# Gated delta heads: decay masks, decayed keys and the rounding of weights on other engines

## The chip, the cores and the metric

The kernel runs on one core of a Trainium2 chip. The metric is the device time of one execution in microseconds (us): the median of 3 runs. Names of engines: PE is TensorE (PEld its weight loads), DVE VectorE, ACT ScalarE, POOL GpSimd, SP SyncE, which issues the DMAs.

## The reference

Two transformer blocks in a row on 1024 tokens of width 1024. The first has neighbourhood attention beside a gated delta rule in both directions; the second has stick-breaking attention beside retention. The change touches the delta rule of the first block, whose core is this:

```python
def _gated_delta_chunked(q, k, v, g, beta):
    g = jnp.cumsum(g, axis=-1)                      # within a chunk
    diff = g[..., :, None] - g[..., None, :]
    decay = jnp.where(tri, jnp.exp(jnp.where(tri, diff, 0.0)), 0.0)
    a_mat = jnp.where(strict, jnp.einsum('bhncd,bhnsd->bhncs', kb, k) * decay, 0.0) + eye
    ...
    intra = jnp.einsum('bhncd,bhnsd->bhncs', q, k) * decay
    ...
    S = S * jnp.exp(g_last) + jnp.einsum('bhcd,bhce->bhde',
                                         k_c * jnp.exp(g_last[..., None] - g_c)[..., None], v_new)
```

The kernel works it in chunks of 128 tokens. There are 4 heads of 128 columns and two directions (`d` is 0 or 1), so 8 pairs, called `dh`.

## The kernel before, in words

All large products are in 32-bit floats split in two: a rounded part (`hi`, float32r) and the residue (`lo`), three matmuls for one product (`PASSES`). Weights come from HBM in units of 128 rows: `split_unit` loads a unit into `raw` (3 slots), writes the rounded part to `wu[:, 0]` (line 70, on POOL) and the residue to `wu[:, 1]` (line 71, on POOL). `wu` has 10 slots; a group of weights is 8 units (`load_units`).

The program is written as one function and put in order by a list scheduler of the framework, which models the engines' times and writes out one fixed order for each engine and for the DMA queue on SP. An engine runs its order strictly in sequence and waits at the head of it.

First come the norm of the input, its transposes (`h1hi`, `h1lo`) and the gates, ending in `gc`, the sum of the log decays within a chunk by token (`[P, 8, NM]`, P = 128 partitions, NM = 8 chunks), and its transposed copy in DRAM, `d_g`.

Then the loop over 4 delta heads (lines 304 to 435), the stage of the change. For a head: 8 units of 3 x 128 columns of weights (line 308); three products with the input (`dense_col`, line 112), each in two halves that ACT copies to `pad` (line 315); the convolution of five taps on DVE (lines 318, 320); silu on ACT (line 323); norms and transposes to `kt`, `vt`, `kT` (lines 327 to 356). For each direction, `G` is the row of the sums, broadcast to all partitions by a DMA (line 370); `el` is the decay to the end of the chunk. The inner function `decay` makes a mask of 128 x 8 x 128: the difference of `G` and the token's own sum (DVE, line 385), the triangle by an affine select (POOL, line 386), the exponential (ACT, line 389). E0, E2 and E1 are such masks; E2 and E1 share a buffer. N (line 406) and IT (line 421) are products of masks with the keys' and queries' products in PSUM, sent to DRAM (`d_N`, `d_pk`). Last, `G` becomes its exponential in place (line 427), and three scaled tiles per direction go to `d_pk`: lines 430 (DVE and POOL) and 434 (DVE, keys times `el`). Their buffers `sct` are two, shared with `vt`.

After the heads a triangular solver in 62 steps runs on DVE and POOL (lines 463, 465), with the neighbourhood attention on PE beside it; then the merges of the solutions, the scan over chunks, and the output product (line 859, from about 740 us). The second block follows.

Of the kernel before, what the change touches and what calls it, by code (L numbers as in the profile page):

```python
# [11 lines left out]
F32 = mybir.dt.float32  # L12
F32R = mybir.dt.float32r
AF = mybir.ActivationFunctionType
ALU = mybir.AluOpType
# [4 lines left out]
P = 128  # L20
# [16 lines left out]
def tile_kernel(ctx: ExitStack, tc: tile.TileContext, I: dict, out: bass.AP, dbg=None, stop=None):  # L37
# [22 lines left out]

    def split_unit(src, ncol, pool=None, tag="wu", parts=1, fast=False, rpool=None):
        raw = (rpool or wraw).tile([P, ncol], F32, tag="raw", name="raw", bufs=8 if rpool else 3)
        dst = raw if parts == 1 else raw.rearrange("p (g c) -> p g c", g=parts)
        nc.sync.dma_start(out=dst, in_=src)
        u = (pool or wpool).tile([P, 2, ncol], F32R, tag=tag, name="wu")
        if fast:
            nc.scalar.copy(out=u[:, 0, :], in_=raw)
            nc.vector.tensor_tensor(out=u[:, 1, :], in0=raw, in1=f32(u[:, 0, :]), op=ALU.subtract)
        else:
            nc.gpsimd.tensor_scalar(out=u[:, 0, :], in0=raw, scalar1=1.0, scalar2=0.0, op0=ALU.mult, op1=ALU.add)  # L70
            nc.gpsimd.tensor_tensor(out=u[:, 1, :], in0=raw, in1=f32(u[:, 0, :]), op=ALU.subtract)  # L71
        return u

    def load_units(w, c0, width, parts=1, stride=0, pool=None, tag="wu", fast=False, rpool=None):
        us = []
        for k in range(NK):
            rows = w[k * P:(k + 1) * P, :]
            if parts == 1:
                src = rows[:, c0:c0 + width]
            else:  # L80
                src = rows[:, c0:c0 + parts * stride].rearrange("p (g s) -> p g s", g=parts)[:, :, :width]
            us.append(split_unit(src, width * parts, pool, tag, parts, fast and k % 2 == 1, rpool))
        return us
# [3 lines left out]
    def bank(tag, w=512):  # L87
        if tag == "a":
            return psA.tile([P, w], F32, tag="a", name="acc")
        return psB.tile([P, w], F32, tag=tag, name="p" + tag, bufs=2 if tag == "z" else 1)  # L90
# [195 lines left out]
    nc.tensor.matmul(pg[:, 32:64], lhsT=trige, rhs=graw[:, 4:8, :], start=True, stop=True)  # L286
    nc.vector.tensor_copy(out=gc, in_=pg[:, 0:64])
    pgt = bank("z")
    nc.tensor.transpose(pgt[:64, 0:P], gc.rearrange("p a b -> p (a b)"), ident)
# [14 lines left out]
    for h in range(4):  # L304
        kt = dn.tile([P, NM, P], F32, tag="kt", name="kt")
        vt = dn.tile([P, NM, P], F32, tag="sct", name="vt", bufs=2)
        kT = dn.tile([P, T], F32, tag="kT", name="kT")
        us = load_units(I["w_in"], 2048 + 128 * h, 128, parts=3, stride=512)
        sT = []
# [57 lines left out]
        for d in range(2):  # L367
# [7 lines left out]
            nc.scalar.activation(out=el[:, dh, :], in_=el[:, dh, :], func=AF.Exp)  # L375
            gb = gc[:, dh, :].unsqueeze(2).to_broadcast([P, NM, P])
            bb = beta[:, dh, :].unsqueeze(2).to_broadcast([P, NM, P])
# [4 lines left out]

            def decay(a, b, sgn, strict, tag):
                E = dn.tile([P, NM, P], F32, tag=tag, name="E")
                nc.vector.tensor_tensor(out=E, in0=a, in1=b, op=ALU.subtract)
                nc.gpsimd.affine_select(out=E, in_=E, pattern=[[0, NM], [sgn, P]],
                                        compare_op=ALU.is_gt if strict else ALU.is_ge, fill=NEG,
                                        base=0, channel_multiplier=-sgn)
                nc.scalar.activation(out=E, in_=E, func=AF.Exp)
                return E  # L390

            if d == 0:
                E0 = decay(G, gb, 1, False, "E0")
                nc.vector.tensor_tensor(out=E0, in0=E0, in1=bb, op=ALU.mult)
            else:
                E2 = decay(gb, G, 1, True, "E1")
                nc.vector.tensor_tensor(out=E2, in0=E2, in1=bb, op=ALU.mult)
                for g in range(2):
# [5 lines left out]
                    for dd_, E in enumerate((E0, E2)):  # L404
# [4 lines left out]
                        for x, (r_, c_) in enumerate(((0, 0), (64, 64), (0, 64))):  # L409
                            nc.sync.dma_start(out=d_N[x, a_:a_ + 4].rearrange("n r c -> r n c"),  # L410
                                              in_=N[r_:r_ + 64, :, c_:c_ + 64])
                E1 = decay(G, gb, -1, False, "E1")
                for g in range(2):
# [11 lines left out]
        for d in range(2):  # L425
            dh, G = d * 4 + h, Gs[d]
            nc.scalar.activation(out=G, in_=G, func=AF.Exp)
            for f, src in enumerate((kT, sT[0])):
                sc_t = dn.tile([P, NM, P], F32, tag="sct", name="sct", bufs=2)
                (nc.gpsimd if f else nc.vector).tensor_tensor(out=sc_t.rearrange("p n c -> p (n c)"), in0=src, in1=G.rearrange("p n c -> p (n c)"),  # L430
                                        op=ALU.mult)
                nc.sync.dma_start(out=d_pk[d, :, :, f, h, :].rearrange("n p c -> p n c"), in_=sc_t)
            sc_t = dn.tile([P, NM, P], F32, tag="sct", name="sct", bufs=2)
            nc.vector.tensor_tensor(out=sc_t, in0=kt, in1=el[:, dh, :].unsqueeze(2).to_broadcast([P, NM, P]), op=ALU.mult)
            nc.sync.dma_start(out=d_pk[d, :, :, 2, h, :].rearrange("n p c -> p n c"), in_=sc_t)
# [898 lines left out]
```

## Time and profile before

| | us |
|---|---|
| median of 3 runs | 2325.04 (2324.49 to 2326.11) |
| profiled execution | 2327.74 |
| its span, first to last instruction | 2326.0 |
| PE busy in the span | 2189.8 (94%) |
| DVE / ACT / POOL busy | 1270.2 / 892.9 / 1205.7 |
| mean granted TensorE clock | 0.979 |

A busy time is the time in which an engine has an instruction under way; matmuls overlap, so a busy PE is not a PE at its peak. The granted clock is a share of 2.4 GHz. A wait is idle time of an engine ahead of an instruction, put down to what ended last before it.

### The profile page before, as it was taken

What the parts mean: (1) busy time and instruction counts of PE and PEld (TensorE: products, weight loads), DVE (VectorE), ACT (ScalarE), POOL (GpSimd) and SP (SyncE); (2) the same over time, 40 slices, a digit from 0 to 9 for tenths busy, and PEclk for the clock granted to TensorE, in tenths of its full rate; (3) what the DMA queues carried; (4) which work ended last, traced back from release to release, by engine and by line L of the source; (5) the groups of instructions that cost most, each with busy time, mean ns of one, the idle gap of its engine ahead of it and who ended that gap; (6) DMA issues with size and microseconds to landing.
All of it is one profiled execution on the core that took longest, in us unless ns stands there. A gap on an engine that the chain in (4) does not pass through costs nothing.

```text
span 2326.0 us, 33731 instructions
## 1 busy us (share of the span) xinstructions
PE 2189.8 (94%) x12197; PEld 1882.5 (81%) x12197; DVE 1270.2 (55%) x2276; ACT 892.9 (38%) x2222; POOL 1205.7 (52%) x1435
## 2 busy tenths in 40 slices
PE   7998888899999989999999999999999999999999
PEld 7777877787898788898888888788888888667887
DVE  4688789834456545565666543416474744343221
ACT  5344334445554235565656543112222222332200
POOL 6667778751004245554456555536364533566531
PEclk9999999999999999999999999999999999999999
DMA  4266820154475421110111113111111123666432
GB/s 129 82 170 166 204 80 26 37 164 133 156 275 207 152 87 46 51 55 27 39 50 55 55 35 115 41 55 46 64 46 64 46 82 101 220 220 206 141 105 108
DMA packets 236487, 240.86 MB, mean 104 GB/s; under 512 B 39776, under 2 KB 173600, under 8 KB 236064
## 3 DMA queue, kind: packets, MB, share of 16 engines
q1 hardware_dynamic: 236320, 238.71, 32.4%
q8 instruction: 96, 1.57, 0.3%
q14 instruction: 71, 0.58, 0.1%
HBM read 167.31 MB, written 71.34 MB: 103 GB/s over the span
## 4 chain that ended last, share of the span: by engine, by line
PE 43%; DVE 8%; POOL 6%; DMA 4%; ACT 3%; issue 3%; SPq 0%; POOLq 0%; ACTq 0%; DVEq 0%
PE acc L112 24%; PE acc L102 9%; PE acc L859 3%; DMA raw<-in_w_in_dram 2%; POOL wu L71 2%; PE po L1062 2%; DVE A L1041 1%; POOL wu L70 1%; DVE A L1036 1%; POOL A L1046 1%; DMA oa<-d_oa 1%; PE pt L1162 1%; PE po L1173 1%; ACT A L1035 1%; DVE ob L132 1%
## 5 line engine op out<-in xcount | busy, mean ns | idle before, releaser
L112 PE MATMUL acc<-h2h,wu 128*128 128x512 f32 x1504 | 461.8, 397 | 5.4 <-ACT lg L956 4.0
L102 PE MATMUL acc<-wu,h2h 128*128 128x384 f32 (+1 forms) x1536 | 375.0, 326 | 8.7 <-DVE sq L988 3.6
L71 POOL TENSOR_TENSOR wu<-raw,wu 128x512 fp32r<-128x512 f32 (+3 forms) x268 | 361.9, 1360 | 5.3
L112 PEld LDWEIGHTS acc<-h2h,wu 128*128 128x128 f32 x1504 | 282.0, 189 | 71.6 <-ACT lg L956 4.9
L70 POOL TENSOR_SCALAR wu<-raw 128x512 fp32r<-128x512 f32 (+3 forms) x268 | 208.1, 780 | 251.1 <-PE acc L112 177.4
L102 PEld LDWEIGHTS acc<-wu,h2h 128*128 128x128 f32 x1536 | 271.4, 193 | 14.2 <-DVE v L1116 3.4
L112 PE MATMUL acc<-h2l,wu 128*128 128x512 f32 x752 | 277.8, 395 | 0.0
L102 PE MATMUL acc<-wu,h2l 128*128 128x384 f32 (+1 forms) x768 | 249.2, 325 | 0.0
L102 PE MATMUL acc<-wu,h1hi 128*128 128x384 f32 (+2 forms) x768 | 191.8, 333 | 13.8 <-DVE kS L518 6.4
L112 PE MATMUL acc<-h1hi,wu 128*128 128x512 f32 x512 | 164.6, 410 | 7.0 <-ACT pad L315 3.8
L112 PEld LDWEIGHTS acc<-h2l,wu 128*128 128x128 f32 x752 | 142.0, 189 | 31.7
L125 POOL TENSOR_SCALAR ss<-ss 128x2 f32<-128x2 f32 (+2 forms) x136 | 40.3, 296 | 215.4 <-ACT sq L982 144.5
L102 PEld LDWEIGHTS acc<-wu,h1hi 128*128 128x128 f32 x768 | 137.2, 195 | 18.3 <-issue 7.7
L102 PEld LDWEIGHTS acc<-wu,h2l 128*128 128x128 f32 x768 | 148.1, 193 | 1.3
L1046 POOL TENSOR_TENSOR A<-Z,A 128x128 f32<-128x128 f32 (+2 forms) x96 | 110.9, 1160 | 65.4 <-DVE A L1041 46.3
L102 PE MATMUL acc<-wu,h1lo 128*128 128x384 f32 (+2 forms) x384 | 126.8, 333 | 0.0
L112 PEld LDWEIGHTS acc<-h1hi,wu 128*128 128x128 f32 x512 | 98.3, 194 | 32.4 <-ACT pad L315 5.4
L126 POOL TENSOR_TENSOR ss<-ss,mhalf 128x2 f32<-128x2 f32 (+2 forms) x136 | 112.2, 825 | 8.6
L112 PE MATMUL acc<-h1lo,wu 128*128 128x512 f32 x256 | 96.3, 405 | 0.0
L1036 DVE SCALAR_TENSOR_TENSOR A<-Z,A 128x128 f32<-128x128 f32 (+2 forms) x96 | 71.8, 755 | 41.6 <-ACT A L1035 40.7
L1062 PE MATMUL po<-wT,v 128*128 128x512 f32 (+3 forms) x288 | 76.5, 363 | 13.9 <-DVE wT L1060 11.1
L112 PE MATMUL acc<-oah,wu 128*128 128x512 f32 x256 | 81.4, 415 | 8.3 <-DVE sg L1234 6.1
(548 smaller groups left out, 4733.0 us busy)
## 6 DMA issues: line engine op xcount, KB each, us to landing
raw<-in_w_in_dram SPq DMA_DIRECT2D x192, 256.0 KB, 2.9
d_pk<-sct SPq DMA_DIRECT2D x24, 512.0 KB, 4.3
raw<-in_w_out_dram SPq DMA_DIRECT2D x40, 256.0 KB, 3.0
wsa<-d_pk SPq DMA_DIRECT2D x16, 512.0 KB, 5.6
wsb<-d_pk SPq DMA_DIRECT2D x16, 512.0 KB, 7.1
d_sg<-lg SPq DMA_DIRECT2D x32, 256.0 KB, 2.6
sg<-d_sg SPq DMA_DIRECT2D x32, 256.0 KB, 4.0
raw<-in_w_in_dram SPq DMA_DIRECT2D x32, 192.0 KB, 2.7
```

The lines of the kernel that those rows point to most:

```text
L70: nc.gpsimd.tensor_scalar(out=u[:, 0, :], in0=raw, scalar1=1.0, scalar2=0.0, op0=ALU.mult, op1=ALU.add)
L71: nc.gpsimd.tensor_tensor(out=u[:, 1, :], in0=raw, in1=f32(u[:, 0, :]), op=ALU.subtract)
L102: nc.tensor.matmul(acc[:, :n], lhsT=hT[a][:, k, m * P:(m + 1) * P], rhs=us[k][:, b, c0:c0 + n], start=(k == 0 and i == 0), stop=(k == NK - ...
L112: nc.tensor.matmul(accs[half], lhsT=us[k][:, b, c0:c0 + P], rhs=hT[a][:, k, half * 512:(half + 1) * 512], start=(k == 0 and i == 0), stop= ...
L125: nc.gpsimd.tensor_scalar(out=dst, in0=src, scalar1=mul, scalar2=eps, op0=ALU.mult, op1=ALU.add)
L126: nc.gpsimd.tensor_tensor(out=dst, in0=dst, in1=mhalf[:, :eshape], op=ALU.pow)
L132: nc.vector.transpose(out=dst[32 * b:32 * b + 32, :, :, 32 * a:32 * a + 32], in_=src[32 * a:32 * a + 32, :, :, 32 * b:32 * b + 32])
L859: nc.tensor.matmul(acc, lhsT=us[k][:, y, (b % 4) * P:(b % 4 + 1) * P], rhs=token_set(mT[x][:, k, 0:T], s), start=(k == 0 and i == 0), stop ...
L1035: nc.scalar.activation(out=A[:, :w], in_=A[:, :w], func=AF.Ln, bias=1.0)
L1036: nc.vector.scalar_tensor_tensor(out=A[:, :w], in0=Z[:, :w], scalar=0.0, in1=A[:, :w], op0=ALU.max, op1=ALU.add)
L1046: nc.gpsimd.tensor_tensor(out=A[:, :w], in0=Z[:, :w], in1=A[:, :w], op=ALU.subtract)
L1062: nc.tensor.matmul(po[:, i0 * P:512], lhsT=v[a][:, c0 // P + kb, :], rhs=wT[b][:, :n], start=(diag and kb == 0 and x == 0), stop=(diag == ...
```

## The change

In `decay` the subtraction on DVE is dropped. The affine select reads `G` directly (with the opposite fill where the sign turns), and the exponential takes the token's sum as its per-partition bias, with the scale -1 where the sign turns. Since the bias is one value per token and chunk, one exponential over 8 chunks becomes eight over one chunk each. `ngc` is a negated copy of `gc` for it. The decayed keys of line 434 become eight scaled copies on ACT. The rounding of the delta heads' weights goes from POOL to ACT (`act=True`); the residue stays on POOL. A setting of the program's DMA scratch memory is made smaller.

```diff
-    def split_unit(src, ncol, pool=None, tag="wu", parts=1, fast=False, rpool=None):
+    def split_unit(src, ncol, pool=None, tag="wu", parts=1, fast=False, rpool=None, act=False):
...
-            nc.gpsimd.tensor_scalar(out=u[:, 0, :], in0=raw, scalar1=1.0, scalar2=0.0, op0=ALU.mult, op1=ALU.add)
+            if act:
+                nc.scalar.copy(out=u[:, 0, :], in_=raw)
+            else:
+                nc.gpsimd.tensor_scalar(out=u[:, 0, :], in0=raw, scalar1=1.0, scalar2=0.0, op0=ALU.mult, op1=ALU.add)
             nc.gpsimd.tensor_tensor(out=u[:, 1, :], in0=raw, in1=f32(u[:, 0, :]), op=ALU.subtract)
...
+    ngc = sm.tile([P, 8, NM], F32, name="ngc")
+    nc.vector.tensor_scalar_mul(out=ngc, in0=gc, scalar1=-1.0)
...
-        us = load_units(I["w_in"], 2048 + 128 * h, 128, parts=3, stride=512)
+        us = load_units(I["w_in"], 2048 + 128 * h, 128, parts=3, stride=512, act=True)
...
-            def decay(a, b, sgn, strict, tag):
+            def decay(neg, sgn, strict, tag):
                 E = dn.tile([P, NM, P], F32, tag=tag, name="E")
-                nc.vector.tensor_tensor(out=E, in0=a, in1=b, op=ALU.subtract)
-                nc.gpsimd.affine_select(out=E, in_=E, pattern=[[0, NM], [sgn, P]],
-                                        compare_op=ALU.is_gt if strict else ALU.is_ge, fill=NEG,
+                nc.gpsimd.affine_select(out=E, in_=G, pattern=[[0, NM], [sgn, P]],
+                                        compare_op=ALU.is_gt if strict else ALU.is_ge, fill=-NEG if neg else NEG,
                                         base=0, channel_multiplier=-sgn)
-                nc.scalar.activation(out=E, in_=E, func=AF.Exp)
+                for n in range(NM):
+                    nc.scalar.activation(out=E[:, n, :], in_=E[:, n, :], func=AF.Exp, scale=-1.0 if neg else 1.0,
+                                         bias=(gc if neg else ngc)[:, dh, n:n + 1])
                 return E
...
-                E0 = decay(G, gb, 1, False, "E0")
+                E0 = decay(False, 1, False, "E0")
...
-                E2 = decay(gb, G, 1, True, "E1")
+                E2 = decay(True, 1, True, "E1")
...
-                E1 = decay(G, gb, -1, False, "E1")
+                E1 = decay(False, -1, False, "E1")
...
-            nc.vector.tensor_tensor(out=sc_t, in0=kt, in1=el[:, dh, :].unsqueeze(2).to_broadcast([P, NM, P]), op=ALU.mult)
+            for n in range(NM):
+                nc.scalar.activation(out=sc_t[:, n, :], in_=kt[:, n, :], func=AF.Copy, scale=el[:, dh, n:n + 1])
...
-    nc = _bacc.Bacc("TRN2", target_bir_lowering=False, num_devices=1)
+    nc = _bacc.Bacc("TRN2", target_bir_lowering=False, num_devices=1, dynamic_dma_scratch_size=1024)
```

The scheduler makes a new order up to the output product; from there on the orders are the same. PE's order up to the last product of the heads holds the same 1225 instructions before and after. Two places follow, word for word. Lines of the changed kernel lie 3 to 6 higher: its L320, L325, L328, L361, L378, L380, L432 and L440 are L315, L320, L323, L356, L373, L375, L427 and L434 of before.

ACT at the turn from head 0 to head 1, before, from the last copy of `kT` of head 0 to the second pair of `pad` copies of head 1:

```order
L356 COPY kT<-po 128x512
L315 COPY pad<-acc 128x512 x2
L373 ACT_TABLE_LOAD
L373 ACTIVATE eS<-G 128x8
L427 ACTIVATE G<-G 128x1024
L323 ACT_TABLE_LOAD
L323 ACTIVATE s<-cv 128x1024
L375 ACT_TABLE_LOAD
L375 ACTIVATE el<-el 128x8
L389 ACTIVATE E<-E 128x1024
L315 COPY pad<-acc 128x512 x2
```

The same stretch of ACT in the changed kernel:

```order
L320 COPY pad<-acc 128x512 x2
L440 ACTIVATE sct<-kt,el 128x128 x8
L71 CAST wu<-raw 128x384 x3
L378 ACT_TABLE_LOAD
L378 ACTIVATE eS<-G 128x8
L328 ACT_TABLE_LOAD
L328 ACTIVATE s<-cv 128x1024
L380 ACT_TABLE_LOAD
L380 ACTIVATE el<-el 128x8
L393 ACTIVATE E<-E,ngc 128x128 x8
L432 ACTIVATE G<-G 128x1024
L320 COPY pad<-acc 128x512 x2
```

Eight scaled copies and three roundings of weights have come between the two pairs of `pad` copies; the exponential of the mask is in eight parts, and `G`'s own exponential stands behind it and no longer ahead of it.

POOL from the first two masks of head 0 on, before, where L70 is the rounding and L71 the residue of head 1's weights:

```order
L386 AFFINE_SELECT E<-E 128x1024 x2
L70 TENSOR_SCALAR wu<-raw 128x384
L71 TENSOR_TENSOR wu<-raw,wu 128x384
L70 TENSOR_SCALAR wu<-raw 128x384
L71 TENSOR_TENSOR wu<-raw,wu 128x384
L70 TENSOR_SCALAR wu<-raw 128x384
L312 MEMSET pad 128x2
L313 MEMSET pad 128x2
L71 TENSOR_TENSOR wu<-raw,wu 128x384
```

And in the changed kernel, where L74 is the residue:

```order
L389 AFFINE_SELECT E<-G 128x1024 x2
L317 MEMSET pad 128x2
L318 MEMSET pad 128x2
L74 TENSOR_TENSOR wu<-raw,wu 128x384 x6
L317 MEMSET pad 128x2
L318 MEMSET pad 128x2
L74 TENSOR_TENSOR wu<-raw,wu 128x384 x2
```

The eight residues of head 1 stand alone on POOL, and the select reads `G` instead of `E`.

## Rows read from the trace of the kernel before

**Rows 1.** Busy by stage: PE, PEld, DVE, ACT, POOL (instructions), PEclk, DMA.

```profile
60.00:290.00 230.00, 208.34 (x1048) 174.91 (x1047) 182.50 (x180) 100.20 (x207) 163.14 (x149) 0.96 0.58 154
290.00:470.00 180.00, 156.31 (x919) 130.90 (x918) 161.01 (x365) 71.37 (x190) 145.12 (x214) 0.95 0.16 48
470.00:740.00 270.00, 263.94 (x2230) 231.31 (x2227) 136.65 (x416) 138.73 (x352) 65.42 (x105) 0.99 0.58 192
740.00:2326.00 1586.00, 1514.02 (x7705) 1301.90 (x7703) 765.27 (x1261) 548.87 (x1406) 794.57 (x909) 0.98 0.26 86
```

**Rows 2.** The same view in slices of 10 us of the heads.

```profile
90.00:100.00 10.00, 9.33 (x39) 7.25 (x40) 6.19 (x5) 1.54 (x4) 9.45 (x13) 0.66 0.29 76
...
250.00:260.00 10.00, 6.03 (x32) 5.27 (x32) 4.07 (x8) 6.93 (x27) 9.52 (x10) 0.88 0.60 150
260.00:270.00 10.00, 9.84 (x54) 9.81 (x55) 7.49 (x14) 2.44 (x7) 6.71 (x8) 0.78 0.54 132
```

**Rows 3.** Waits of PE, 50 to 300 us: total us, times, longest.

```profile
PE po L355 <- DVE kt L346: 5.1, 5, 3.4
PE acc L112 <- ACT pad L315: 3.8, 3, 2.0
PE acc L514 <- DVE kn L506: 3.5, 2, 3.0
PE acc L102 <- ACT pad L315: 2.9, 1, 2.9
...
PE acc L112 <- POOL wu L71: 2.8, 2, 2.1
...
PE acc L102 <- POOL wu L71: 1.4, 1, 1.4
```

**Rows 4.** Timeline of PE at head 1: start, us, what, idle before.

```profile
85.68 0.39 PE L112 MATMUL acc<-h1lo,wu 128*128 128x512 f32 x1
...
86.38 0.40 PE L112 MATMUL acc<-h1lo,wu 128*128 128x512 f32 x1
...
89.85 0.84 PE L112 MATMUL acc<-h1hi,wu 128*128 128x512 f32 x2 [2.10 <-POOL wu L71]
...
93.23 1.05 PE L112 MATMUL acc<-h1hi,wu 128*128 128x512 f32 x2
...
94.51 1.05 PE L112 MATMUL acc<-h1hi,wu 128*128 128x512 f32 x2
```

**Rows 5.** Groups by form, 50 to 300 us: busy us, mean ns, idle before.

```profile
L71 POOL TENSOR_TENSOR wu<-raw,wu 128x384 fp32r<-128x384 f32 x25 | 35.9, 1452 | 0.4
L70 POOL TENSOR_SCALAR wu<-raw 128x384 fp32r<-128x384 f32 x25 | 27.1, 1096 | 13.3 <-PE acc L112 13.2
...
L434 DVE TENSOR_TENSOR sct<-kt,el 128x1024 f32<-128x1024 f32 x8 | 12.8, 1595 | 5.2 <-DMA d_pk<-sct 5.2
...
L385 DVE TENSOR_TENSOR E<-G,gc 128x1024 f32<-128x1024 f32 x8 | 11.4, 1423 | 0.0
...
L385 DVE TENSOR_TENSOR E<-gc,G 128x1024 f32<-128x1024 f32 x4 | 4.8, 1211 | 0.0
```

**Rows 6.** ACT: two lines' durations (ns min/median/max), and four timeline rows.

```profile
L389 ACT ACTIVATE E<-E x12: 1040/1062/1077, 72.5 to 277.0; 128x1024 f32<-128x1024 f32 x12
...
L67 ACT CAST wu<-raw x44: 607/621/652, 723.8 to 1316.4; 128x512 fp32r<-128x512 f32 x44
...
29.51 0.48 ACT L170 ACTIVATE h1hi<-pz,c_norm_w 128x256 fp32r<-128x256 f32 x1
29.87 0.48 ACT L170 ACTIVATE h1hi<-pp,c_norm_w 128x256 fp32r<-128x256 f32 x1
...
250.41 0.29 ACT L501 COPY qn<-acc 128x128 f32<-128x128 f32 x1
250.56 0.32 ACT L502 COPY kn<-acc 128x128 f32<-128x128 f32 x1
```

**Rows 7.** Waits of DVE, 60 to 300 us: total us, times, longest.

```profile
DVE sct L434 <- DMA d_pk<-sct: 5.2, 2, 3.0
```

More of the change, by code (lines that the diff above doesn't have):

```diff
@@ L69, in split_unit, with load_units @@
         else:
-            nc.gpsimd.tensor_scalar(out=u[:, 0, :], in0=raw, scalar1=1.0, scalar2=0.0, op0=ALU.mult, op1=ALU.add)
+            if act:
+                nc.scalar.copy(out=u[:, 0, :], in_=raw)
+            else:
+                nc.gpsimd.tensor_scalar(out=u[:, 0, :], in0=raw, scalar1=1.0, scalar2=0.0, op0=ALU.mult, op1=ALU.add)
             nc.gpsimd.tensor_tensor(out=u[:, 1, :], in0=raw, in1=f32(u[:, 0, :]), op=ALU.subtract)
         return u
-    def load_units(w, c0, width, parts=1, stride=0, pool=None, tag="wu", fast=False, rpool=None):
+    def load_units(w, c0, width, parts=1, stride=0, pool=None, tag="wu", fast=False, rpool=None, act=False):
         us = []
@@ L81, in load_units @@
                 src = rows[:, c0:c0 + parts * stride].rearrange("p (g s) -> p g s", g=parts)[:, :, :width]
-            us.append(split_unit(src, width * parts, pool, tag, parts, fast and k % 2 == 1, rpool))
+            us.append(split_unit(src, width * parts, pool, tag, parts, fast and k % 2 == 1, rpool, act))
         return us
@@ L375, in tile_kernel @@
             nc.scalar.activation(out=el[:, dh, :], in_=el[:, dh, :], func=AF.Exp)
-            gb = gc[:, dh, :].unsqueeze(2).to_broadcast([P, NM, P])
             bb = beta[:, dh, :].unsqueeze(2).to_broadcast([P, NM, P])
```

## The prediction

> **What bounds the kernel now.** I read the table by stages first [rows 1]. Columns are busy us of PE, PEld, DVE, ACT and POOL with counts, then the granted clock. From 740 us on PE works 1514 of 1586 us, and the order of instructions there is the same in both kernels, so that stretch only shifts. From 470 to 740 PE works 264 of 270 us: it has enough to do and a delay there is short. The change lies in the delta heads, 60 to 290 us. There PE works 208.3 of 230 us at a mean clock of 0.96: 21.7 us of gaps, and 230 x 0.04 = 9.2 us lost to the lower clock. Some 31 us is therefore all that this stage can give back on PE. DVE is next with 182.5 us (79%), POOL has 163.1 (71%), ACT only 100.2 (44%). From 290 to 470 DVE carries the solver and is busy 161 of 180 us; the change leaves no work out there.
>
> Next the waits of PE in the heads [rows 3]: kt from DVE 5.1 us, the copies of pad from ACT 3.8 and 2.9, kn from DVE 3.5, the weights from POOL 2.8 and 1.4. Then what a gap does to the clock [rows 2, 4]. Before the gap three matmuls of 512 columns take 0.70 us (85.68 to 86.38); PE then stands 2.10 us for POOL's residue and from there three take 1.28 us (93.23 to 94.51): near the 1.2 GHz level instead of 2.4. The slice 90 to 100 has a mean of 0.66, that is 3.4 us lost on top of the gap; 250 to 270 has 0.88 and 0.78, again 3.4 us. So a gap costs about double.
>
> **The change part by part.**
>
> *Decay masks.* Twelve subtractions on DVE go: 8 x 1.423 + 4 x 1.211 = 16.2 us [rows 5]. The mask on POOL now reads G itself, with the same size, so it costs POOL what it did. On ACT one exponential of 1024 columns (1.062 us) becomes eight of 128 with a per-partition bias. No row shows that shape. From above and below: 256 columns with a per-partition scale start 0.36 us apart (29.51 to 29.87), plain copies of 128 columns 0.15 us apart (250.41 to 250.56) [rows 6]. The bias is a pointer as the scale is, so I lean to the first and take off the 128 columns that are missing at the 1062/1024 = 1.04 ns a column of the long form: 0.23, called 0.25 for the bias that is new. Eight take 2.0 us, bounds 1.2 and 2.9. Twelve masks: 12 x (2.0 - 1.06) = +11.3 us on ACT, bounds +1.7 to +22. One negated copy of gc, 128x64 on DVE, lies beside PE's first weights; no cover would make it some 0.2 us.
>
> *Decayed keys.* Eight products on DVE go, 8 x 1.595 = 12.8 us [rows 5]; 64 scaled copies of 128 columns come on ACT, 8 x 2.0 = +16 us (bounds 9.6 to 23). Their wait for a free sct buffer, 5.2 us in two places on DVE [rows 7], moves to ACT's queue with them. SP issues the same stores and loads; a store of decayed keys now waits for ACT instead of DVE, and the loads of raw weights queued behind it on SP with it, while raw slots come free sooner, since POOL works a unit in 1.45 us (below).
>
> *Weight rounding.* POOL loses 32 roundings of 384 columns, 1.10 us each [rows 5]; 25 of them lie in the window of the row, 27.1 us, the others are head 0's, ahead of the stage. ACT gains 32 x 0.5 = 16 us, half a microsecond being the 0.621 us of the same cast at 512 columns less 128 columns [rows 6]. A unit needs 1.10 + 1.45 = 2.55 us of POOL before and 1.45 after, beside ACT's 0.5. PE eats a unit in six matmuls, 1.40 us at full clock [rows 4]. Before, POOL falls behind by more than 1 us a unit; after, the two are level.
>
> Engine sums for 60 to 290: DVE 182.5 - 29 = 153.5, POOL 163 - 27 = 136, ACT 100 + 43 = 143, PE's work unchanged. Only ACT rises, to about two thirds of the stage.
>
> The Trainium skill, ScalarE: Activation LUTs, section What ACT_TABLE_LOAD costs, gives an ACTIVATE with a pointer operand 280 ns + 0.833 ns a column, less 93 ns for neighbours. That makes 0.40 us for the 256 columns of rows 6, where the trace has 0.36, and 0.29 us for 128; ACT would gain some 7 us more than I count. The measurement decides for my value, and by the page's price the sum would move by under half a microsecond.
>
> What of this is on the path, as lost time of PE:
> 1. POOL starves PE at head 1: 2.8 us of gap and the 3.4 us of low clock behind it. POOL is level with PE afterwards, so I take -6.0 (bounds 0 to -6.2).
> 2. The weights of na_proj, still rounded on POOL, wait 1.4 us at 240 to 250 [rows 3]; POOL is 27 us less busy ahead of them. I take half, -0.7 (0 to -1.4).
> 3. PE waits for DVE (kt 5.1, kn 3.5) with 3.4 us of low clock at 250 to 270: 12.0 us. DVE sheds 29 of 182.5 us, a sixth of its queue, and the operations that remain reach kt and kn sooner; but kt also hangs on POOL's inverse root and ACT's squares. I take -7.5 (0 to -12).
> 4. PE waits for ACT's pad copies, 6.7 us. ACT's busy share grows from 0.44 to about 0.66, so these waits grow by half; I take +3.0 (0 to +6.7).
> 5. The solver stretch starts earlier by what the heads give, and its own length stays: 0, with -2 to +4 for another interleaving of the attention with it.
>
> Sum -6.0 - 0.7 - 7.5 + 3.0 = -11.2 us. The profiled execution took 2327.74 us with a span of 2326.0, 1.7 us around it, and stands 2.7 above the median of 2325.04. What is taken off lies inside the span, so I take it from the median: 2313.8, called **2313.5**. Likeliest case by its bounds: 2303 to 2320.
>
> **The rivals.**
>
> *Slower: ACT becomes what PE waits for.* ACT runs in order, and in the order of the changed kernel eight scaled copies and three roundings stand between the pad copies of head 0's end and those of head 1, where there was neither. The scaled copies wait for a store to free sct (3.0 us at worst, [rows 7]) and the roundings for PE to release weight slots; the silu, the exponentials and the pad copies queue behind them, and PE waits for pad. One such place costs 3.0 + 2.0 + 1.5 = 6.5 us of gap and 3.4 of low clock, 9.9 us; there are about seven, two a head less the last. Without step 4 the gain is 14.2, so it is gone from the second place on: with two, 2325 - 14.2 + 19.8 = 2330.6. For it: the pad copies are already 6.7 us of PE's waits. Against it: ACT has 130 us of idle time in the stage, and three accumulator banks give PE one product of cover.
>
> The Trainium skill, ScalarE: Activation LUTs, section Rules for kernel authors, sends products to VectorE and not to ScalarE, and by that rule the decayed keys go the wrong way. The rows agree on the time of one (2.0 on ACT against 1.6 on DVE), which would be 8 x 0.4 = 3.2 us lost if engine time alone counted; no rows here say that it does, since DVE is the busier engine.
>
> *No change.* The relief comes off the path. DVE idles 47.5 of 230 us already [rows 1], and in the new order its second IT product waits for eight exponentials that stand behind a load of G and two table loads on ACT. Then only step 1 is left and step 4 takes half of it: -6.0 + 3.0 = -3, 2322.
>
> *A larger gain.* If the heads run at DVE's pace, all 29 us come through: 2296. Against it: PE's own gaps and clock are only 31 us, and nothing makes it run without gaps.
>
> **How the numbers follow.** Forecast 0.49, larger gain 0.13, no change 0.20, slower 0.18. A measurement of this kernel tells about 0.2% (4.6 us) from no change. The forecast and the larger gain are faster: 0.62; same 0.20; slower 0.18. The range 2297 to 2331 takes the forecast's bounds, the no-change case, half of the larger gain (down to 2297) and half of the slower case (up to 2331).
>
> **What would show it.** Step 1: the wait of PE for POOL's residue at head 1 is gone and the slice after it is at full clock. Step 3: PE's waits for kt and kn halve, DVE's busy time in the heads is near 153 us. Step 4: PE's waits for pad stay under 10 us. Stage: the solver's stretch begins 8 to 16 us earlier than 290 us, and the output product at 740 us is earlier by as much. Price: eight exponentials take 1.2 to 2.9 us. It is wrong if PE's gaps in the heads stay at 20 us or more, or if the solver starts earlier and the start of the output product does not.

## The result, and the profile after

The changed kernel takes 2340.89 us (median of 4 runs, 2340.1 to 2342.44), the kernel before in the same comparison 2325.57. The ratio is 1.0058 with a 95% interval of 1.0042 to 1.0073, or 13.5 us slower. The forecast was 2313.5, with a range up to 2331. Both the sign and the range were wrong.

The stages after, in the columns of [rows 1] (PE, PEld, DVE, ACT, POOL busy with instructions, granted clock, DMA):

```profile
60.00:290.00 230.00, 207.29 (x1009) 175.32 (x1008) 147.80 (x152) 136.86 (x356) 128.57 (x121) 0.92 0.53 143
290.00:470.00 180.00, 153.66 (x872) 127.96 (x872) 160.93 (x351) 68.30 (x189) 139.24 (x199) 0.92 0.21 59
```

The engine sums lie below what was worked out: DVE 147.8 (153.5 was forecast), POOL 128.6 (136), ACT 136.9 (143). But less work was done in the window: PE ran 1009 matmuls from 60 to 290 us where it had run 1048, with the same idle time (22.7 us, before 21.7) and a mean clock of 0.92 instead of 0.96. So the relief of DVE and POOL did not reach PE. Cut at the kernels' own marks (the solver's first step, then the output product), the same view reads, for the kernel before:

```profile
60.00:293.70 233.70, 209.74 (x1053) 175.77 (x1051) 183.09 (x181) 100.20 (x207) 163.14 (x149) 0.96 0.58 153
293.70:719.90 426.20, 398.75 (x2994) 343.29 (x2995) 282.89 (x748) 200.86 (x512) 198.99 (x296) 0.98 0.41 132
```

and for the changed kernel:

```profile
60.00:303.20 243.20, 215.67 (x1042) 182.14 (x1041) 152.61 (x159) 140.23 (x367) 133.30 (x126) 0.92 0.55 145
303.20:739.00 435.80, 407.28 (x3003) 348.16 (x3003) 284.41 (x750) 205.11 (x520) 198.58 (x296) 0.96 0.40 129
```

Up to the solver, where the same work is done, the sums are close to the forecast: DVE 152.6, POOL 133.3, ACT 140.2. Yet the solver starts 9.5 us later, and the stretch behind it, whose work did not change, is 9.6 us longer. PE's idle time over both stages is 51.4 us before and 56.0 after.

The low clock is length times what is missing to 1. Two decimals over such long stretches are coarse for it, so I add it up over slices of 5 us: 8.5 + 10.2 = 18.7 us before and 19.6 + 15.3 = 34.9 after. That is 16.2 us more low clock beside 4.6 us more gaps; counting only the share of the low clock in which PE was busy, it is 12.8 us more (29.0 against 16.2). Of what PE lost over both stages, about three quarters is therefore clock and not gaps. The timed runs agree: the mean clock is 0.974 over the four runs of the changed kernel (0.972 to 0.976) and 0.979 over 29 runs of the kernel before (0.975 to 0.985), which is some 12 us.

(From the output product on, the profiled execution of before was 6.7 us longer than that of the changed kernel, 1606.1 against 1599.4, with the same work. Single executions differ by that much, so verdicts rest on the timed runs; two executions of 2410 and 4217 us, of other kernels below, were disturbed and are left out.)

PE's waits, 50 to 300 us, answering to [rows 3] (total us, times, longest):

```profile
PE acc L115 <- ACT pad L320: 6.4, 4, 3.0
PE pp L422 <- DVE IT L426: 6.0, 2, 4.8
PE acc L105 <- ACT v L509: 4.2, 1, 4.2
...
PE pp L422 <- DVE rq L336: 2.7, 1, 2.7
PE acc L105 <- POOL wu L73: 2.3, 2, 1.4
PE pz L346 <- DVE rq L336: 1.5, 1, 1.5
...
PE acc L105 <- POOL wu L74: 0.9, 1, 0.9
```

The waits for kt and for the residue at head 1 are gone. The waits for pad are no longer than before (6.4 us, before 6.7), and those for the weights of na_proj not shorter (2.3 + 0.9, before 1.4 + 1.4). What is new are the waits for IT, the attention's v and an inverse root (rq). What ACT waits for, 60 to 320 us:

```profile
ACT sct L440 <- DMA d_pk<-sct: 19.0, 5, 10.6
...
ACT sct L440 <- issue: 7.1, 2, 3.7
```

and POOL:

```profile
POOL wu L74 <- ACT wu L71: 26.2, 7, 10.2
```

The wait for a free sct buffer was 5.2 us on DVE [rows 7] and is now over 19 on ACT. The residue on POOL waits 26.2 us for ACT's rounding. One place, from the timeline of the changed kernel, shows how scaled copies on ACT reach PE:

```profile
202.53 0.17 DVE L338 TENSOR_SCALAR rq<-rq 128x8 f32<-128x8 f32 x1 [4.31 <-POOL rq L129]
...
202.84 2.44 ACT L440 ACTIVATE sct<-kt,el 128x128 f32<-128x128 f32 x8 [3.74 <-issue]
...
205.19 1.05 ACT L320 COPY pad<-acc 128x512 f32<-128x512 f32 x2
205.39 0.69 DVE L351 TENSOR_TENSOR kt<-pz,ks 128x512 f32<-128x512 f32 x1 [2.68 <-ACT sct L440]
205.81 0.80 PE L115 MATMUL acc<-h1hi,wu 128*128 128x512 f32 x1 [3.03 <-ACT pad L320]
```

ACT stands 3.74 us at the scaled copies, the pad copies are behind them, and PE waits 3.03 us for pad. What ACT waited for here the profile does not show ("issue"), so this place is not known to be the wait for a store. In slices of 10 us, answering to [rows 2], the one with this gap has PE busy 6.97 us at a clock of 0.67, and others are as low with PE busy 9 us and more:

```profile
90.00:100.00 10.00, 9.06 (x45) 7.09 (x44) 7.33 (x7) 5.30 (x15) 5.78 (x9) 0.78 0.31 80
...
200.00:210.00 10.00, 6.97 (x26) 5.67 (x26) 4.59 (x7) 5.90 (x17) 5.32 (x9) 0.67 1.07 305
240.00:250.00 10.00, 9.43 (x48) 9.43 (x49) 8.45 (x9) 3.42 (x10) 10.00 (x7) 0.71 1.02 280
260.00:270.00 10.00, 9.25 (x40) 9.22 (x41) 5.40 (x13) 6.00 (x30) 7.27 (x12) 0.68 0.20 47
```

Prices, 60 to 303 us by lines of ACT (busy us, mean ns of a record, idle before):

```profile
L393 ACT ACTIVATE E<-E,ngc 128x128 f32<-128x128 f32 x64 | 19.6, 389 | 9.6 <-POOL E L389 9.6
L440 ACT ACTIVATE sct<-kt,el 128x128 f32<-128x128 f32 x56 | 17.1, 389 | 15.5 <-DMA d_pk<-sct 8.4 <-issue 7.1
...
L71 ACT CAST wu<-raw 128x384 fp32r<-128x384 f32 x22 | 10.9, 511 | 11.9 <-DMA raw<-in_w_in_dram 7.5 <-PE acc L115 4.3
```

Eight exponentials take 19.6/8 = 2.45 us (2.0 was taken, 2.9 the upper bound), eight scaled copies the same, a rounding 0.50 (0.5 was taken). For an ACTIVATE with a pointer operand the estimate by the Trainium skill, ScalarE: Activation LUTs, section What ACT_TABLE_LOAD costs, was 0.29 us each, 2.35 for eight. The measured 0.306 is nearer to it than to my 0.25.

### The profile page after: what moved, and what is told of

Read it like the earlier page. It is cut to its first block, busy times and chain, and to the rows that moved or that the text cites. A ratio compares the mean times of both kernels' runs of the same rounds, so it can differ in the third digit from the quotient of the medians.

```text
span 2338.4 us, 33898 instructions
## 1 busy us (share of the span) xinstructions
PE 2201.9 (94%) x12197; PEld 1892.7 (81%) x12197; DVE 1240.4 (53%) x2257; ACT 942.1 (40%) x2402; POOL 1171.0 (50%) x1403
## 4 chain that ended last, share of the span: by engine, by line
PE 55%; DVE 14%; POOL 10%; DMA 8%; ACT 7%; issue 6%; SPq 0%; POOLq 0%; ACTq 0%; DVEq 0%
PE acc L115 24%; PE acc L105 13%; PE acc L865 3%; POOL wu L74 3%; DMA raw<-in_w_in_dram 3%; PE po L1068 2%; POOL wu L73 1%; DVE svt L469 1%; DVE X L471 1%; DVE A L1047 1%; POOL ss L129 1%; DMA oa<-d_oa 1%; PE pz L558 1%; DVE A L1042 1%; DVE ob L135 1%
## 5 line engine op out<-in xcount | busy, mean ns | idle before, releaser
L74 POOL TENSOR_TENSOR wu<-raw,wu 128x512 fp32r<-128x512 f32 (+3 forms) x268 | 361.4, 1358 | 36.4 <-ACT wu L71 31.4
L73 POOL TENSOR_SCALAR wu<-raw 128x512 fp32r<-128x512 f32 (+2 forms) x236 | 179.2, 762 | 245.7 <-PE acc L115 162.2
L105 PE MATMUL acc<-wu,h1hi 128*128 128x384 f32 (+2 forms) x768 | 198.8, 341 | 11.2 <-ACT v L509 4.2
L105 PEld LDWEIGHTS acc<-wu,h2l 128*128 128x128 f32 x768 | 147.8, 192 | 1.3
```

Of the source, the lines that this page charges most:

```text
L105: nc.tensor.matmul(acc[:, :n], lhsT=hT[a][:, k, m * P:(m + 1) * P], rhs=us[k][:, b, c0:c0 + n], start=(k == 0 and i == 0), stop=(k == NK - ...
```

## The experiments

**Which part.** The setting of the scratch memory alone, then each part alone with the order that the scheduler writes for it.

```diff
+    nc = _bacc.Bacc("TRN2", target_bir_lowering=False, num_devices=1, dynamic_dma_scratch_size=1024)
```

> The kernel before with the smaller DMA scratch memory alone; the order of instructions on every engine is that of the kernel before. All theories on the heads (keys, weights, masks) expect 2325 us, within 2 us. If the setting itself cost time, it would be up to 2341 us, and the 15 us would have nothing to do with the engines.

Ratio 0.9992 (0.9978 to 1.0006): the setting costs nothing.

The decayed keys on ACT alone:

```diff
-            nc.vector.tensor_tensor(out=sc_t, in0=kt, in1=el[:, dh, :].unsqueeze(2).to_broadcast([P, NM, P]), op=ALU.mult)
+            for n in range(NM):
+                nc.scalar.activation(out=sc_t[:, n, :], in_=kt[:, n, :], func=AF.Copy, scale=el[:, dh, n:n + 1])
```

> Decayed keys on ACT alone; masks and weights as before. Theory K (ACT stands in its order at the scaled copies, which wait for the store that frees their sct buffer, and pad copies, silu and exponentials queue behind): slower by 8 to 15 us, 2333 to 2340, with ACT's wait for d_pk<-sct at 10 us or more. Theory W (the residue on POOL waits for ACT's rounding) and theory M (masks in eight exponentials hold ACT): faster by 0 to 6 us, 2319 to 2325, since DVE sheds 12.8 us. Theory O (each edit makes the scheduler write another order, and orders differ by chance): any change up to 10 us either way, unlike the sum of the parts.

Ratio 1.0014 (1.0001 to 1.0026), 3.3 us, with 6.6 us of ACT waiting for sct. Theory K missed, since it wanted 8 us or more, and so did W and M, which wanted a gain; theory O, any change up to 10 us either way, allows it but is hard to miss.

The rounding alone:

```diff
-        us = load_units(I["w_in"], 2048 + 128 * h, 128, parts=3, stride=512)
+        us = load_units(I["w_in"], 2048 + 128 * h, 128, parts=3, stride=512, act=True)
```

> Rounding of the delta heads' weights on ACT alone. Theory W: slower by 5 to 12 us, 2330 to 2337, with POOL's residue waiting 15 us or more for ACT's rounding and PE's waits for weights or pad longer. Theories K and M: faster by 3 to 6 us, 2319 to 2322, since POOL no longer starves PE at head 1. Theory O: up to 10 us either way.

Ratio 1.0022 (1.0011 to 1.0033), 5 us, with POOL waiting 18.9 us for the roundings: the low edge of theory W.

The masks alone (the change of `decay` and `ngc`, as in the diff ahead):

> Masks alone: select on G, eight exponentials with the bias on ACT; keys on DVE, weights on POOL. Theory M: slower by 5 to 12 us, 2330 to 2337, with ACT's pad copies late for PE. Theories K and W: faster by 2 to 8 us, 2317 to 2323, since DVE sheds 16 us. Theory O: up to 10 us either way. In each of the four runs the theories also say where: PE's loss from 60 us to the start of the output product is gaps and low clock in the heads, not more work.

Ratio 1.0052 (1.0036 to 1.0068), 12 us: by size, the masks are nearly all of it. But the three parts together would be 20 us and not 13.5, and in this kernel DVE has 20 us less to do up to the solver (162.95 against 183.09), which still starts 16 us later than before (309.6; the profiled execution was the slowest of six, 2348.6 against a median of 2340.6). So the next question was whether the instructions cost it, or the order that the scheduler writes with them.

**Order against instructions.** In the next kernels the order of every engine and of SP's queue is given: a table of places (ORDER) is read, and each instruction is tied behind the one that precedes it on its engine. The ties carry no semaphore (`NoSync`), and two kernels pinned in this way ran at 1.0003 and 0.9998, so pinning itself costs nothing that can be seen.

```diff
+        for _k in np.cumsum(_d):
+            _i = _ins[int(_k)]
+            _p = _last.get(str(_i.engine))
+            if _p is not None:
+                tc.add_manual_dep(_i, _p.name, mybir.DependencyInfo(mybir.DependencyClass.NoSync, mybir.DependencyReason.DATA), reason="order")
+            _last[str(_i.engine)] = _i
```

> The changed kernel's instructions, pinned in the kernel before's order on every engine and on SP's queue: what the change replaces stands where the replaced instruction stood in the scheduler's list (eight exponentials for one, a mask's select without its subtraction, eight scaled copies on ACT in the place of the product on DVE, the rounding on ACT in the place of the rounding on POOL). Theory O (the new order costs the time, the instructions themselves are cheap): 2310 to 2322 us. Theory C (the instructions cost it: ACT's longer exponentials and the waits that move to ACT): 2332 to 2345 us in this order too.

> The kernel before's instructions, pinned in the changed kernel's order on every engine and on SP's queue; a subtraction on DVE stands right before its select, a product of keys and a rounding where the changed kernel has them on ACT. Theory O: slower than before by 8 to 20 us, 2333 to 2345. Theory C: 2322 to 2330 us, since the instructions are those of before.

> Masks alone (select on G, eight exponentials with the bias), pinned in the kernel before's order. Alone with an order of its own the masks took 2341 us. Theory O: 2316 to 2325 us. Theory C (eight exponentials hold ACT by 17 us in the heads): 2332 to 2341 us.

> Decayed keys on ACT alone, pinned in the kernel before's order. All of the change in that order gave 2326.8, the masks 2327.5. Theory A (ACT's longer work ahead of the pad copies eats what the other engines gain): the scaled copies take ACT 20 us but stand at the end of a head, so 2322 to 2326 us. Rival (the store that frees sct holds the pad copies also in this order): 2328 to 2335 us.

> Rounding of the delta heads' weights on ACT alone, pinned in the kernel before's order. Theory A: the part of the change that pays, since a rounding holds ACT for only 0.5 us and POOL no longer starves PE at head 1: 2315 to 2321 us. Rival (the residue on POOL waits for ACT's turn as it did in the changed kernel): 2326 to 2333 us.

All ratios to the kernel before:

| instructions | in the order written for them | in the order of before |
|---|---|---|
| keys | 1.0014 (1.0001 to 1.0026) | 1.0003 (0.9992 to 1.0014) |
| weights | 1.0022 (1.0011 to 1.0033) | 0.9998 (0.9985 to 1.0012) |
| masks | 1.0052 (1.0036 to 1.0068) | 1.0008 (0.9995 to 1.0020) |
| all three | 1.0058 (1.0042 to 1.0073) | 1.0008 (0.9999 to 1.0016) |
| those of before, in the changed kernel's order | 1.0113 (1.0099 to 1.0126) | 1 |

The loss is in the order: with the old one the whole change costs nothing that can be told from 0, and with the new one the old instructions are 26 us slower (more than the 8 to 20 expected). Theory C fell, and theory O held in its direction. But the gain that it expected in the old order did not come: 2310 to 2322 was expected for all three and 2316 to 2325 for the masks, where 2326.8 and 2327.5 were measured. Theory A missed for the weights too (2323.1, where 2315 to 2321 was expected); for the keys 2324.1 lies in its range. The table says two more things. In the new order the change is worth 1.0113 - 1.0058, 0.55% or 13 us. That this is near the forecast's 11.2 us is luck: it is measured against the old instructions in an order that was not written for them. In the old order the change is worth nothing. Its stages there:

```profile
60.00:294.90 234.90, 207.86 (x1052) 176.85 (x1050) 154.68 (x161) 144.59 (x377) 126.44 (x127) 0.96 0.57 152
294.90:720.30 425.40, 400.76 (x2995) 345.00 (x2995) 281.78 (x748) 200.92 (x512) 198.78 (x296) 0.97 0.41 132
```

and PE's waits, 50 to 300 us:

```profile
PE acc L117 <- ACT pad L322: 9.4, 5, 3.9
PE acc L107 <- ACT v L511: 5.3, 1, 5.3
PE acc L107 <- ACT pad L322: 4.4, 1, 4.4
PE acc L522 <- DVE kn L514: 3.5, 2, 2.5
...
PE acc L117 <- ACT v L511: 1.5, 1, 1.5
...
PE acc L107 <- POOL wu L76: 0.2, 1, 0.2
```

Here one sees the trade in one order, so wait by wait. Against [rows 3], kt fell from 5.1 us to nothing, POOL's from 5.6 (2.8, 1.4 and another 1.4 for a rounding) to 0.2; kn stayed at 3.5. That is 10.5 us of relief. The waits for pad grew from 6.7 to 13.8 and those for v from 1.1 to 6.8: 12.8 us. PE's idle time up to the solver is 27.0 us, before 24.0. Two of these rows of before were not shown ahead:

```profile
PE acc L102 <- POOL wu L70: 1.4, 1, 1.4
PE acc L102 <- ACT v L503: 1.1, 1, 1.1
```

The timeline of ACT, and of PE in the last row, at one of them in the third head:

```profile
197.24 1.06 ACT L434 ACTIVATE G<-G 128x1024 f32<-128x1024 f32 x1 [1.47 <-POOL E L391]
198.20 2.43 ACT L395 ACTIVATE E<-E,ngc 128x128 f32<-128x128 f32 x8
200.53 1.04 ACT L322 COPY pad<-acc 128x512 f32<-128x512 f32 x2
...
201.15 0.80 PE L117 MATMUL acc<-h1hi,wu 128*128 128x512 f32 x1 [3.84 <-ACT pad L322]
```

The exponential of G now waits for POOL's select, which has become the last reader of G; eight exponentials follow, and only then the pad copies for which PE has stood 3.84 us.

**What in ACT's work.** The pad copies were put ahead at the four worst places, in ACT's order alone; at the one just shown:

```diff
-L434 ACTIVATE G<-G 128x1024
-L395 ACTIVATE E<-E,ngc 128x128 x8
 L322 COPY pad<-acc 128x512 x2
+L434 ACTIVATE G<-G 128x1024
+L395 ACTIVATE E<-E,ngc 128x128 x8
```

> The changed kernel's instructions in the kernel before's order (2326.8 us as it was), with four changes in ACT's order alone: the pad copies of head 1's second pair ahead of el and the exponentials, those of head 2's third load ahead of G's exponential and the mask's, those of head 3 ahead of the scaled copies, and the first two groups of the attention's sq, qn, kn, v ahead of G's exponential. At these four places PE had waited 3.9, 3.8, 4.4 and 5.3 us. Theory A (ACT's longer work ahead of what PE waits for ate the gain): 2310 to 2319 us. Rival P (the gaps only move to the next wait, since PE waits for several chains that are about as late): 2322 to 2327 us.

Ratio 1.0010 (0.9994 to 1.0025), 2329.46 us: no gain. The waits for pad fell to 0.8 us and others took their place:

```profile
PE pp L424 <- DVE IT L428: 5.4, 2, 4.0
PE po L362 <- DVE kt L353: 5.2, 2, 2.7
...
PE pz L337 <- ACT sq L334: 2.7, 2, 1.8
...
PE acc L117 <- ACT pad L322: 0.8, 1, 0.8
```

Rival P is right that other waits grew, but not that PE stood as long. Its idle time up to the solver fell from 27.0 to 21.8 us:

```profile
60.00:297.70 237.70, 215.90 (x1056) 183.76 (x1054) 156.55 (x162) 145.00 (x377) 127.10 (x127) 0.93 0.57 151
```

The solver started later all the same (297.7 us, without the move 294.9), while the low clock up to there went from 8.8 to 17.6 us (added over slices of 5 us). The timed runs point the same way: the mean clock is 0.975 over 12 runs with the copies ahead and 0.978 over 11 without. Fewer gaps bought no time here; why the clock was lower is not shown. The length of the work itself was tried next, with one exponential a mask:

```diff
-                for n in range(NM):
-                    nc.scalar.activation(out=E[:, n, :], in_=E[:, n, :], func=AF.Exp, scale=-1.0 if neg else 1.0,
-                                         bias=(gc if neg else ngc)[:, dh, n:n + 1])
+                nc.scalar.activation(out=E, in_=E, func=AF.Exp, scale=-0.001 if neg else 0.001)
```

> The changed kernel's instructions in the kernel before's order, with one exponential of 1024 columns a mask instead of eight of 128; the token's own sum is left out of the mask, and its row is scaled by 0.001 so that the values stay finite. ACT has some 16 us less to do. Theory A: 2312 to 2320 us. Rival P: 2322 to 2327 us.

Ratio 0.9968 (0.9956 to 0.9981), 2320.19 us, the edge of what theory A gave. Against 1.0008 with eight exponentials in the same order, twelve times 2.45 - 1.06 = 1.39, or 16.7 us of ACT, are worth 0.40%, 9 us (each ratio is to the kernel before on the same chip, but the two chips differ). The solver starts at 290.7 us instead of 294.9, and the output product at 719.8 instead of 720.3:

```profile
60.00:290.70 230.70, 208.47 (x1056) 178.06 (x1055) 150.47 (x161) 128.54 (x293) 128.34 (x127) 0.96 0.58 155
290.70:719.80 429.10, 401.56 (x2995) 344.77 (x2995) 282.75 (x748) 200.62 (x512) 199.13 (x296) 0.97 0.41 131
```

In the profiled executions the 4.2 us of the heads are thus gone again by the output product, and PE's waits for pad and v fell only from 20.6 to 17.8 us. The traces do not show where the 9 us of the timed runs come from. This kernel also works with other values in the masks, and that these have no effect on the time was not tested. So the runs speak for theory A, that ACT's longer work costs time, but do not prove its path.

**Does any new order cost?** An unused negated copy of gc, then eight unused small copies on POOL (below) or on DVE:

```diff
+            nc.gpsimd.tensor_scalar(out=ngc[:, dh, :], in0=kt[:, 0, 0:NM], scalar1=1.0, scalar2=0.0, op0=ALU.mult, op1=ALU.add)
```

> The kernel before with one more instruction, the negated copy of gc, which nothing reads: 128x64 on DVE ahead of the heads. The scheduler writes another order for it on every engine. Theory O: the time may move by 3 to 12 us either way, though the work is the same. Theory C: within 2 us of before, 2323.5 to 2327.5.

> The kernel before with eight unused copies of 8 columns on POOL, one a pair of head and direction, ahead of G's exponential. The scheduler's order changes with them: 1860 of 11243 matmuls stand elsewhere (2544 in the changed kernel). Theory O (the kernel before has an uncommonly good order, and any other costs): slower by 5 to 16 us, 2329 to 2340. Rival (what costs is that these instructions are moved to ACT, and a list order fits its own work): within 3 us of before.

> The kernel before with eight unused copies of 8 columns on DVE, one a pair of head and direction. 593 of 11243 matmuls stand elsewhere. Theory O: slower by 2 to 10 us, 2326 to 2334. Rival: within 3 us of before.

The premise of the first was wrong: compared place by place, the order did not change at all, and the ratio is 1.0005 (0.9994 to 1.0016). The other two do change it, and cost nothing: 1.0001 (0.9989 to 1.0013) with 1860 matmuls elsewhere, 1.0008 (0.9993 to 1.0023) with 593. So it is not true that any new order costs. But these two orders begin to differ from the kernel before's only at PE's 1129th and 1125th matmul, near 266 us; up to there they are the same, while the changed kernel's differs from the 100th on. Whether the kernel before's order is a lucky one in the heads is therefore not tested. From PE's 2420th matmul on (538 us in the changed kernel), its order with the copies on POOL and its order in the changed kernel are the same. The costly part of the new order lies ahead of that: in the heads and beside the solver.

**Where in the new order.** The changed kernel's instructions, its own order in one stretch and that of before in the others:

> The changed kernel's instructions; up to the solver's first step pinned in the changed kernel's own order, from there on in the kernel before's. Theory S (the new order costs in both stages, about 9.5 us in the heads by the start of the solver and 9.6 between it and the output product): solver starts at 303 us, output product 426 later at 729, total 2329 to 2335 us. Theory H (all of it comes from the heads; the later stretch only inherits late work): output product near 739 again, total 2338 to 2343.

> The changed kernel's instructions; up to the solver's first step pinned in the kernel before's order, from there on in the changed kernel's own. Theory S: solver starts at 295 us, output product 435 later at 730, total 2333 to 2339 us. Theory H: output product near 720, total 2325 to 2328 us.

> The changed kernel's instructions; in the changed kernel's own order up to TensorE's 875th matmul (the end of head 1), from there on in the kernel before's. All in the order of before: ratio 1.0008; the whole of the heads in its own order: 1.0040. Theory D (the own order costs a little at many places): about half of that 0.3%, ratio 1.002 to 1.003, 2328 to 2332 us. Theory L1 (it costs at one place in heads 0 and 1, where the second products of masks came 18 us later): 1.004 or more, 2333 us or more. Theory L2 (at one place in heads 2 and 3): 1.000 to 1.001, 2324 to 2327 us.

> The changed kernel's instructions; in the kernel before's order up to TensorE's 875th matmul, then the rest of the heads in the changed kernel's own order, and from the solver's first step on in the kernel before's again. Theory D: ratio 1.002 to 1.003, 2328 to 2332 us. Theory L1: 1.000 to 1.001, 2324 to 2327 us. Theory L2: 1.004 or more, 2333 us or more.

| own order in | ratio |
|---|---|
| heads 0 to 3 | 1.0040 (1.0026 to 1.0055) |
| heads 0 and 1 | 1.0036 (1.0023 to 1.0048) |
| heads 2 and 3 | 1.0024 (1.0011 to 1.0037) |
| what follows the heads | 1.0067 (1.0055 to 1.0080) |

No trace of the last row is read here. Each stretch costs by itself, and both halves of the heads do: theories L1 and L2, one bad place, fall (L1 only by the second half), and theory D is the nearest, though the first half (1.0036) is above the 1.002 to 1.003 that it gave. The parts don't add up (1.0040 and 1.0067 against 1.0058 for all): perhaps a stretch of the new order fits the state in which the stretch before it ends, which is not shown. Nor is the loss of every stretch low clock: with the own order in heads 0 and 1 the mean clock of the timed runs is 0.978, that of the kernel before 0.979, and the trace has 31.1 us of idle time up to the solver (24.0 before):

```profile
60.00:302.60 242.60, 211.42 (x1054) 179.04 (x1052) 150.07 (x163) 139.41 (x373) 133.64 (x127) 0.95 0.56 149
```

Where the heads kept the new order and the rest the old one, the solver started at 301.2 us and the output product at 727.3:

```profile
60.00:301.20 241.20, 211.68 (x1046) 179.44 (x1046) 150.81 (x163) 137.28 (x365) 132.80 (x126) 0.93 0.56 148
301.20:727.30 426.10, 402.27 (x3004) 346.37 (x3002) 280.76 (x748) 203.61 (x520) 197.97 (x296) 0.97 0.41 133
```

The second stretch is back at 426 us, as theory S said: it does not inherit late work from the heads. The times, 2332.2 and 2339.2 us, lie within theory S's 2329 to 2335 and at the upper edge of its 2333 to 2339; theory H fell.

## Why the prediction was wrong

The steps that failed are 1 to 3, which counted 14.2 us of ended waits as gain, step 4, which put 3.0 us against it where 12.8 was measured in the old order, and step 5, which put the new order beside the solver at 0 where it cost 9.6 in the profiled executions. Four signs that the prediction named came true all the same: waits for kt and kn halved (8.6 us before, 1.8 up to 310 us after), DVE's 153 us, pad under 10 us, and a price within its bounds. Its sign of being wrong came true too, PE's gaps above 20 us (22.7).

**Step 1** (POOL at head 1, -6.0) and **step 2** (-0.7): in the old order the waits went, from 5.6 to 0.2 us. In the changed kernel that of step 1 went and that of step 2 did not (3.2 us, before 2.8; the prediction had left out the 1.4 us that stood at the rounding). But the slices from 90 to 110 us are at 0.78 and 0.88 in the changed kernel, without a gap of the old kind (see the last section), and rounding on ACT alone in the old order gave 0.9998. The step took the end of a wait for a gain of time; PE had it back at the next late result. It also priced the clock by the rule that a gap costs about double. That rule came from two places, and the heads as a whole do not bear it out: 21.7 us of gaps stand there with 9.2 us of low clock, and the slice with nearly the most idle time of all, not shown ahead, was at full clock:

```profile
240.00:250.00 10.00, 6.45 (x37) 5.45 (x35) 10.00 (x10) 6.53 (x18) 9.84 (x8) 1.00 0.94 250
```

**Step 3** (kt and kn, -7.5): kt went to nothing, and DVE's sum was right; kn stayed at 3.5 us in the old order. The relief was spent in the same way: in the changed kernel PE waits 6.0 us for IT and 4.2 for rq (2.7 and 1.5), all from DVE, which has 30 us less to do up to the solver but itself waits for ACT and POOL (at 202.53 us it had stood 4.31 us for POOL's rq).

**Step 4** (ACT's pad copies, +3.0, upper bound 6.7) is the term that was mis-sized in the old order. In the changed kernel pad stands at 6.4 us, and the price was paid elsewhere. In the one order in which it can be read wait by wait, pad grew by 7.1 and v, which the step did not name, by 5.7: 12.8 us, more than the 10.5 that steps 1 to 3 set free. "Waits grow with the busy share" was the wrong rule: 144.6 of 234.9 us is no full engine, but what PE waits for is a short copy behind a long row of jobs, and the row got longer by 1.4 us a mask and by a wait for POOL's select. The price of eight exponentials was low by a fifth (2.0 for 2.45 us), within its bounds.

**Step 5** (the solver's stretch, 0, up to +4) failed with 9.6 us, where the old order keeps the stretch's length (425.4 us, before 426.2). There was no step at all for the order of the heads, and low clock was counted only behind a gap. Together these are the 0.50% between 1.0008 and 1.0058. I had looked at the new order at two places for what it moved and taken the rest as neutral.

**The range.** Its upper end did not follow from the steps: their own upper bounds, +6.7 and +4 with no relief, add up to 2335.7, not to the 2320 of the likeliest case, and the 2331 came from half of the slower rival.

**The rivals.** "Slower" came true in sign. Something like its mechanism is in the trace (3.74, then 3.03 us at 203 to 206, though not put down to a store), but its two places give 2330.6 us. With the keys alone on ACT in the old order, ACT waited 12.0 us for sct and the ratio was 1.0003:

```profile
ACT sct L440 <- DMA d_pk<-sct: 12.0, 5, 4.0
```

So it can be one of several chains, but such a wait need not cost anything. The Trainium skill, ScalarE: Activation LUTs, section Rules for kernel authors, sends products to VectorE and not to ScalarE. Keys on ACT are 1.0014 and 1.0003; no run here shows a gain from breaking the rule. "No change" is what the old order shows: the relief comes off the path, though there by pad and v and not by IT.

**Open.** Why the new order draws nearly twice the low clock with nearly the same idle time (34.9 against 18.7 us, 56.0 against 51.4) is not settled. No single place holds it, and no run held the clock fixed. No version with the whole computation beat the kernel before.

## What to carry to other kernels

A wait that ends earlier is no gain until the next late result is named: sum the chains behind the bound engine, and charge work that moves to an in-order engine with what queues behind it, not with the engine's free share. Where a scheduler writes the order, price order and instructions apart by pinning the old order on the new instructions and the reverse; here the instructions were worth 0 and 0.55% in the two orders and the order cost 0.5 to 1.1%. Count low clock as a term of its own and not as a fixed surcharge on gaps: it was about three quarters of what PE lost in the changed kernel, though not in every order that was tried.

## What was not expected of the hardware

The clock also fell where PE had hardly stood. At the start of head 1 in the changed kernel the timeline marks no idle time of PE from 85.67 to 97.78 us. PE ran pairs of 512-column matmuls in 0.63 us, then sixteen matmuls of two columns for 1.95 us and four transposes, and from there a pair took 1.05 us:

```profile
92.26 0.63 PE L115 MATMUL acc<-h1hi,wu 128*128 128x512 f32 x2
...
93.50 1.95 PE L335 MATMUL pz<-ones,sq 128*128 128x2 f32 x16
95.31 0.77 PE L346 MATMUL pz<-ident,s 128*128 128x128 f32 x4
...
96.73 1.05 PE L115 MATMUL acc<-h1hi,wu 128*128 128x512 f32 x2
...
140.44 1.84 PE L335 MATMUL pz<-ones,sq 128*128 128x2 f32 x16
```

The pair at 96.73 is at the 1.2 GHz level. That the small matmuls ahead of it brought the clock down is not shown: the same sixteen ran again at 140.44 us, after 1.8 us of idle time between 132 and 136, and the granted clock stayed at 1.00 from 104 to 150 us. So in this trace neither idle time nor the kind of matmul alone tells where the clock falls, and a busy share of 9.06 of 10 us did not keep the slice from 90 to 100 us at full clock (0.78).
